# A QKV projection on one core: the first two row tiles of x loaded, cast and turned one by one, and the next work re-ordered around them

## Chip, cores, metric

One core of one Trainium2 chip. The metric is the device time of one execution in microseconds (us).

## The reference

```python
# x: 16 x 512 x 768 fp32, w_qkv: 768 x 2304 fp32
qkv = np.matmul(x, w_qkv)
q, k, v = qkv[..., :768], qkv[..., 768:1536], qkv[..., 1536:]
return np.stack([q, k, v], axis=0).astype(np.float32)
```

x is 8192 rows of 768 columns. A "row tile" is 128 rows, a "pair" two of them; there are 32 pairs. The 768 inner columns are six k-tiles of 128.

## The kernel before

The kernel has a start, which this change touches, and a long even part, which it does not. In the even part (pairs 3 to 31) the products are done in a seven-product scheme on 2 x 2 blocks, with TensorE nearly always busy. At the start the weights for that scheme are not there yet, so pairs 0 to 2 are multiplied plainly, block of weight columns by block, while the weights stream in. Rows of x must be cast to bf16 and turned (TensorE transposes through PSUM) before they can be a stationary operand. While nothing has landed, TensorE multiplies zeros ("warm-ups"), meant to have its clock at full rate when the work comes: in the trace of the kernel before these matmuls start 0.427 us apart at first and 0.216 us apart after 6.4 us.

```python
    def load_rows(p):                    # one load of 768 KB: a pair of x
        xin[p] = xin_pool.tile([P, 2, K], fp32, name="xin")
        rows = x_flat[p * 2 * P:(p + 1) * 2 * P, :]
        nc.sync.dma_start(xin[p][:], rows.rearrange("(r m) k -> m r k", m=P))

    def copy_halves(dst, src, two):      # VectorE takes a half, ScalarE the other
        nc.vector.tensor_copy(out=dst[0], in_=src[0])
        if two:
            nc.scalar.activation(dst[1], src[1], ident)
        else:
            nc.vector.tensor_copy(out=dst[1], in_=src[1])
    ...
    load_rows(0)
    ...
    load_rows(1)
    load_blocks(0, 0, 1)                 # six k-tiles of the first weight block, 256 KB each
    st_rem = o_pool.tile([P, KT, REM], fp32, name="str", tag="o")
    load_w(st_rem[:], 0, KT, R_OFF, REM) # weights of the 256 remainder columns, 768 KB
    load_rows(2)
    load_blocks(0, 1)
    ...
    busy(11)                             # warm-up matmuls on zeros
    cast_rows(0)
    turn_rows(0)
    busy(4)
    cast_rows(1)
    cast_k(0)
    cast_k(1)
    turn_rows(1)
    ...
    block(0, 0, b1[0], singles, nothing) # pairs 0 and 1 by the first weight block
    rem(0)                               # remainder columns of pair 0, 12 matmuls
    rem(1)
    cast_rows(2, False)
    turn_rows(2, False)
    block(0, 0, b1[0], halves((4, 5)), nothing)   # pair 2
    ...                                  # second weight block: never idle from here on
```

The schedule is written by hand: each engine runs its instructions in the order of the program. All loads shown go out on SyncE's queue.

## Time and profile before

| | before |
|---|---|
| time, median of 6 runs (those beside the changed kernel) | 362.96 us (362.75 to 363.25) |
| profiled span | 361.4 us |
| second pair of x has landed | 7.03 us |
| third pair of x has landed | 15.31 us |
| first product (TensorE) | 9.19 us |
| first product with the second weight block | 20.54 us |

The landings are read from the trace, which records when each load's semaphore is raised. The prediction below shows the page, the chain and the timeline. One more view: the table by stretches. Its columns are the stretch in us, its length, then for each engine the busy time and the number of instructions (PE, PEld, DVE, ACT, POOL), then the granted clock of TensorE, the mean busy share of the 16 DMA engines, and what they moved in GB/s.

### The profile page before, as it was taken

What the parts mean: (1) busy time and instruction counts of PE and PEld (TensorE: products, weight loads), DVE (VectorE), ACT (ScalarE), POOL (GpSimd) and SP (SyncE); (2) the same over time, 40 slices, a digit from 0 to 9 for tenths busy, and PEclk for the clock granted to TensorE, in tenths of its full rate; (3) what the DMA queues carried; (4) which work ended last, traced back from release to release, by engine and by line L of the source; (5) the groups of instructions that cost most, each with busy time, mean ns of one, the idle gap of its engine ahead of it and who ended that gap; (6) DMA issues with size and microseconds to landing.
All of it is one profiled execution on the core that took longest, in us unless ns stands there. A gap on an engine that the chain in (4) does not pass through costs nothing.

```text
span 361.4 us, 5220 instructions
## 1 busy us (share of the span) xinstructions
PE 353.3 (98%) x1765; PEld 250.8 (69%) x1797; DVE 222.7 (62%) x239; ACT 182.5 (51%) x304; POOL 174.4 (48%) x180
## 2 busy tenths in 40 slices
PE   8999999999999999999999999999999999999994
PEld 3644577777777777777777777777777777777763
DVE  3489546666566765566675565676556676556642
ACT  4547555455454545454545444445545454545452
POOL 0000970566664445664445665444666444566410
PEclk9999999999999999999999999999999999999999
DMA  7999969799899989999999999898999998989766
GB/s 294 381 383 338 348 227 345 271 354 304 279 322 298 296 275 296 282 313 314 284 278 295 282 306 316 284 276 291 295 285 317 295 296 276 297 279 331 267 251 242
DMA packets 80617, 108.08 MB, mean 299 GB/s; under 512 B 4816, under 2 KB 60368, under 8 KB 80592
## 3 DMA queue, kind: packets, MB, share of 16 engines
q1 hardware_dynamic: 65184, 96.35, 82.3%
q10 hardware_dynamic: 15408, 11.41, 9.9%
q8 instruction: 14, 0.23, 0.3%
q14 instruction: 11, 0.09, 0.1%
HBM read 32.24 MB, written 75.50 MB: 298 GB/s over the span
## 4 chain that ended last, share of the span: by engine, by line
PE 96%; ACT 1%; issue 1%; ACTq 0%; DVE 0%
PE ps L206 75%; PE ps L256 11%; PE ps L382 9%; PE ps L362 1%; PE ps L161 1%; ACT o L237 0%; ACTq L297 0%; ACT xb L141 0%; ACT orem L311 0%; DVE xb L139 0%; ACT xc L141 0%; ACTq L313 0%; DVE zero L340 0%; ACTq L311 0%
## 5 line engine op out<-in xcount | busy, mean ns | idle before, releaser
L206 PE MATMUL ps<-t,s 128*128 128x512 f32 x696 | 173.8, 398 | 0.0
L206 PEld LDWEIGHTS ps<-t,s 128*128 128x128 f32 x696 | 130.7, 188 | 29.8
L169 POOL CAST xb<-xf 128x1536 bf16<-128x1536 f32 x29 | 46.4, 1601 | 167.7 <-DVE xf L124 167.7
L234 DVE TENSOR_TENSOR o<-o,ps 128x512 f32<-128x512 f32 x58 | 39.9, 688 | 87.6 <-ACT o L233 87.6
L124 DVE STREAM_TRANSPOSE xf<-xin 128x1536 f32<-128x1536 f32 x29 | 85.7, 2956 | 9.7 <-DMA xin<-in_x_dram 7.1
L206 PE MATMUL ps<-b,xb 128*128 128x512 bf16 x320 | 82.4, 380 | 1.5
L233 ACT ACTIVATE o<-ps 128x512 f32<-128x512 f32 x58 | 34.7, 598 | 44.3 <-PE ps L206 44.3
L206 PEld LDWEIGHTS <-xb 128*128 128x128 bf16 x348 | 31.7, 98 | 35.6 <-issue 7.6
L227 ACT ACTIVATE o<-ps 128x512 f32<-128x512 f32 x58 | 34.8, 600 | 40.0 <-PE ps L206 37.3
L240 DVE TENSOR_TENSOR o<-o,ps 128x512 f32<-128x512 f32 x58 | 39.9, 688 | 21.4 <-PE ps L206 20.2
L206 PE MATMUL ps<-b,s 128*128 128x512 f32 x174 | 48.7, 389 | 0.0
L256 PE MATMUL ps<-w_rem,xb 128*128 128x256 bf16 x384 | 47.2, 273 | 0.0
L237 ACT ACTIVATE o<-ps 128x512 f32<-128x512 f32 x58 | 34.7, 598 | 24.1 <-PE ps L206 21.3
L220 ACT ACTIVATE o<-ps 128x512 f32<-128x512 f32 x58 | 34.6, 597 | 23.8 <-DVE o L240 20.7
L256 PEld LDWEIGHTS <-xb 128*128 128x128 bf16 x384 | 37.4, 98 | 11.2 <-issue 0.5
L224 DVE TENSOR_TENSOR o<-o,ps 128x512 f32<-128x512 f32 x58 | 36.5, 673 | 3.4 <-PE ps L206 2.1
L206 PEld LDWEIGHTS ps<-b,s 128*128 128x128 f32 x174 | 32.7, 188 | 6.8
L178 POOL TENSOR_TENSOR s<-s,xf 128x384 fp32r<-128x384 f32 x29 | 29.5, 1016 | 2.3
L266 ACT ACTIVATE orem<-ps 128x512 f32<-128x512 f32 x31 | 18.6, 598 | 22.7 <-PE ps L256 21.4
L179 POOL TENSOR_TENSOR s<-xf 128x384 fp32r<-128x384 f32 x29 | 29.5, 1017 | 0.0
L181 POOL TENSOR_TENSOR s<-xf,s 128x384 fp32r<-128x384 f32 x29 | 29.4, 1015 | 0.0
L177 POOL TENSOR_TENSOR s<-xf 128x384 fp32r<-128x384 f32 x29 | 29.3, 1012 | 0.0
(36 smaller groups left out, 127.2 us busy)
## 6 DMA issues: line engine op xcount, KB each, us to landing
out_dram<-o SPq DMA_DIRECT2D x62, 768.0 KB, 5.1
out_dram<-o SPq DMA_DIRECT2D x65, 256.0 KB, 4.6
xin<-in_x_dram SPq DMA_DIRECT2D x62, 192.0 KB, 6.7
xin<-in_x_dram ACTq DMA_DIRECT2D x54, 192.0 KB, 4.5
out_dram<-orem SPq DMA_DIRECT2D x31, 256.0 KB, 5.5
st<-in_w_qkv_dram SPq DMA_DIRECT2D x6, 768.0 KB, 14.1
xin<-in_x_dram SPq DMA_DIRECT2D x3, 768.0 KB, 5.8
st<-in_w_qkv_dram SPq DMA_DIRECT2D x6, 256.0 KB, 6.3
```

The source lines that it names most:

```text
L124: nc.vector.transpose(t[:].rearrange("p j (g b) -> p g j b", b=G), xin.pop(p)[:].rearrange("p g (a j) -> p g j a", a=G),)
L169: nc.gpsimd.tensor_copy(out=xb[p][:], in_=xf[p][:])
L206: nc.tensor.matmul(ps[:], lhs[j], rhs[j], start=(start and j == 0), stop=(j == KH - 1), skip_group_check=True,)
L220: nc.scalar.activation(c11, u.x[:], ident)
L224: nc.vector.tensor_tensor(c11, c11, u.z[:], op=add)
L227: nc.scalar.activation(c12, u.x[:], ident)
L233: nc.scalar.activation(c22, u.x[:], ident)
L234: nc.vector.tensor_tensor(c22, c22, u.y[:], op=add)
L237: nc.scalar.activation(c21, u.x[:], ident)
L240: nc.vector.tensor_tensor(c12, c12, u.y[:], op=add)
L256: nc.tensor.matmul(ps, xb[p][:, j, r * P:(r + 1) * P], w_rem[:, j, :], start=(j == 0), stop=(j == KT - 1), skip_group_check=True,)
L382: nc.tensor.matmul(ps[n][:], xb[p][:, j, r * P:(r + 1) * P], w[:, j, :], start=(j == 0), stop=(j == KT - 1), skip_group_check=True,)
```

## The change

The intent is to start sooner. The first row tile arrives alone, so that its cast and turn can begin a microsecond earlier; the second pair's first row is turned before its second; its second turn is put behind the two products with the first k-tile; the remainder's weights come in two halves and VectorE alone casts them; and each remainder is followed by the cast and turn of one row of the third pair. The core of the diff:

```diff
+    def load_row(p, r):
+        if r == 0:
+            xin[p] = xin_pool.tile([P, 2, K], fp32, name="xin")
+        row = (2 * p + r) * P
+        nc.sync.dma_start(xin[p][:, r, :], x_flat[row:row + P, :])
 ...   (cast_rows and turn_rows become cast_row and turn_row, one row tile each)
-    load_rows(0)
+    load_row(0, 0)
 ...
+    load_row(0, 1)
     load_rows(1)
-    load_blocks(0, 0, 1)
+    for j in range(KT):
+        load_k(j)
-    load_w(st_rem[:], 0, KT, R_OFF, REM)
+    for h in range(2):
+        load_w(st_rem[:, h * KH:(h + 1) * KH], h * KH, KH, R_OFF, REM)
 ...
-    busy(11)
-    cast_rows(0)
-    turn_rows(0)
-    busy(4)
-    cast_rows(1)
-    cast_k(0)
-    cast_k(1)
-    turn_rows(1)
+    busy(8)
+    cast_row(0, 0)
+    cast_row(0, 1)
+    turn_row(0, 0)
+    busy(1)
+    turn_row(0, 1)
+    busy(5)
+    cast_row(1, 0)
+    cast_row(1, 1)
+    cast_k(0)
+    turn_row(1, 0)
+    # products of k-tile 0 with pair 0, then: cast_k(1), turn_row(1, 1), the other casts
 ...
-    rem(0)
-    rem(1)
-    cast_rows(2, False)
-    turn_rows(2, False)
-    block(0, 0, b1[0], halves((4, 5)), nothing)
+    for p in range(2):
+        rem(p)
+        cast_row(2, p, False)
+        turn_row(2, p, False)
+    block(0, 0, b1[0], [(range(KT), (4, )), (range(KT), (5, ))], nothing)
```

More of the change, by code (lines that the diff above doesn't have):

```diff
@@ L145, with cast_row, turn_row @@
     xc = {}
-    def cast_rows(p, two=True):
-        src = xin.pop(p)
-        xc[p] = s_pool.tile([P, 2, K], bf16, name="xc", tag="s")
-        for r in range(2):
-            halves = (slice(0, K // 2), slice(K // 2, K))
-            copy_halves([xc[p][:, r, n] for n in halves], [src[:, r, n] for n in halves], two)
-    def turn_rows(p, two=True):
-        c = xc.pop(p)
-        xb[p] = xb_pool.tile([P, KT, 2 * P], bf16, name="xb")
-        for r in range(2):
-            cols = c[:, r, :].rearrange("m (p j) -> m j p", j=KT)
-            ps = ps_pool.tile([P, KT, P], bf16, name="ps")
-            for j in range(KT):
-                nc.tensor.transpose(ps[:, j, :], cols[:, j, :], eye)
-            ks = (slice(0, KH), slice(KH, KT))
-            copy_halves(
-                [xb[p][:, n, r * P:(r + 1) * P] for n in ks], [ps[:, n, :] for n in ks], two
-            )
+    def cast_row(p, r, two=True):
+        if r == 0:
+            xc[p] = s_pool.tile([P, 2, K], bf16, name="xc", tag="s")
+        halves = (slice(0, K // 2), slice(K // 2, K))
+        copy_halves([xc[p][:, r, n] for n in halves], [xin[p][:, r, n] for n in halves], two)
+    def turn_row(p, r, two=True):
+        if r == 0:
+            xb[p] = xb_pool.tile([P, KT, 2 * P], bf16, name="xb")
+        cols = xc[p][:, r, :].rearrange("m (p j) -> m j p", j=KT)
+        ps = ps_pool.tile([P, KT, P], bf16, name="ps")
+        for j in range(KT):
+            nc.tensor.transpose(ps[:, j, :], cols[:, j, :], eye)
+        ks = (slice(0, KH), slice(KH, KT))
+        copy_halves(
+            [xb[p][:, n, r * P:(r + 1) * P] for n in ks], [ps[:, n, :] for n in ks], two
+        )
     def round_x(p):
@@ L346, with load_k @@
     make_identity(nc, eye)
+    st_0 = tq_pool.tile([P, KT, CB], fp32, name="st0", tag="tq")
+    stage[0, 0, 0], stage[0, 1, 0] = st_0[:, :KH, :], st_0[:, KH:, :]
+    def load_k(j):
+        load_w(st_0[:, j:j + 1], j, 1, Q_OFF[0], CB)
+    load_row(0, 1)
     load_rows(1)
-    load_blocks(0, 0, 1)
+    for j in range(KT):
+        load_k(j)
     st_rem = o_pool.tile([P, KT, REM], fp32, name="str", tag="o")
-    load_w(st_rem[:], 0, KT, R_OFF, REM)
+    for h in range(2):
+        load_w(st_rem[:, h * KH:(h + 1) * KH], h * KH, KH, R_OFF, REM)
     load_rows(2)
-    load_blocks(0, 1)
+    load_blocks(0, 1, KH)
     load_blocks(1, 0)
@@ L375, in block @@
         ps = {}
-        for js, tiles in groups:
+        for group in groups:
+            if callable(group):
+                group()
+                continue
+            js, tiles = group
             for n in tiles:
@@ L396, in halves @@
         return [(range(h * KH, (h + 1) * KH), tiles) for h in range(2)]
-    singles = [((0, ), (0, 1)), ((1, ), (0, 1)), ((0, 1), (2, 3))]
-    singles += [((j, ), range(4)) for j in range(2, KT)]
     act, dve = nc.scalar, nc.vector
-    def cast_k(j):
-        dve.tensor_copy(out=b1[0][:, j, :], in_=stage[0, j // KH, 0][:, j % KH, :])
     def cast_next(q, c, w):
@@ L412, with fourth_row @@
     nothing = lambda p: None
-    busy(11)
-    cast_rows(0)
-    turn_rows(0)
-    busy(4)
-    cast_rows(1)
-    cast_k(0)
-    cast_k(1)
-    turn_rows(1)
-    for j in range(2, KT):
-        cast_k(j)
-    act.activation(w_rem[:, KH:], st_rem[:, KH:], ident)
-    dve.tensor_copy(out=w_rem[:, :KH], in_=st_rem[:, :KH])
+    busy(8)
[7 more added lines that the diff above has]
+    cast_row(1, 1)
+    cast_k(0)
+    turn_row(1, 0)
+    def fourth_row():
+        cast_k(1)
+        turn_row(1, 1)
+        for j in range(2, KT):
+            cast_k(j)
+        for h in range(2):
+            ks = slice(h * KH, (h + 1) * KH)
+            dve.tensor_copy(out=w_rem[:, ks], in_=st_rem[:, ks])
     bt0 = bt_pool.tile([P, KT, CB], bf16, name="bt")
     bt1 = bt_pool.tile([P, KT, CB], bf16, name="bt")
-    block(0, 0, b1[0], singles, nothing)
-    rem(0)
-    rem(1)
-    cast_rows(2, False)
-    turn_rows(2, False)
-    block(0, 0, b1[0], halves((4, 5)), nothing)
+    block(
+        0, 0, b1[0],
+        [((0, ), (0, 1)), fourth_row, ((1, ), (0, 1)), ((0, 1), (2, )), ((0, 1), (3, ))]
+        + [((j, ), range(4)) for j in range(2, KT)],
+        nothing,
+    )
+    for p in range(2):
[3 more added lines that the diff above has]
+    block(0, 0, b1[0], [(range(KT), (4, )), (range(KT), (5, ))], nothing)
     for h in range(2):
```

## The prediction

> **What bounds the kernel now.** I read the page first, for the engine that sets the pace, then its chain of work that ended last, then that chain in order of time for the first 21 us, which is the only stretch the change touches, and last the timeline by engine there.
>
> ```profile
> PE 353.3 (98%) x1765; PEld 250.8 (69%) x1797; DVE 222.7 (62%) x239; ACT 182.5 (51%) x304; POOL 174.4 (48%) x180
> ...
> PE 96%; ACT 1%; issue 1%; ACTq 0%; DVE 0%
> ```
>
> TensorE is busy 98% of a span of 361.4 us and carries 96% of the chain. So a change is worth what it moves TensorE's uninterrupted stream of work. The table by stretches has TensorE busy 23.36 of the 23.46 us from 20.54 us (the first product with the second block of weights) to 44 us; VectorE comes next with 19.10, and the chain there is matmuls alone. Whatever is won or lost before 20.54 us is carried unchanged to the end. The chain in order of time, 6 to 21 us (start, length, what):
>
> ```profile
> 6.06 0.59 PE ps L161 x6
> 6.65 0.02 issue
> 6.67 0.37 DVE xb L139
> 7.04 0.02 issue
> 7.07 0.87 ACT xb L141 x2
> 7.94 0.42 ACT xc L141
> 8.36 0.05 issue
> 8.40 0.95 PE ps L161 x12
> 9.35 2.16 PE ps L382 x10
> ...
> 14.53 2.62 PE ps L256 x24
> 17.15 0.35 PE ps L161 x6
> 17.50 0.02 issue
> 17.53 0.37 DVE xb L139
> 17.89 0.05 issue
> 17.94 0.39 PE ps L382
> ```
>
> L161 are the turns (PE transposes) of x, L382 the products of the first blocks, L256 those of the remainder columns. The reader is to see one long detour off TensorE, 6.65 to 8.40 us: ScalarE must copy the first pair's turned halves (0.87 us) before it casts the second pair, and TensorE stands still for the 0.57 us that the timeline gives ahead of the second turn. From 8.40 us on TensorE is on the path again and waits only once, about 0.28 us before 17.94.
>
> The timeline shows two loads that will matter (start, length, engine, what, idle before it):
>
> ```profile
> 7.04 0.39 SPq L135 DMA_DIRECT2D xin<-in_x_dram  x1
> 13.37 0.56 DVE L424 CAST w_rem<-str 128x768 bf16<-128x768 f32 x1 [1.83 <-DMA str<-in_w_qkv_dram]
> 15.43 0.36 DVE L139 CAST xc<-xin 128x384 bf16<-128x384 f32 x1 [1.50 <-DMA xin<-in_x_dram]
> ```
>
> VectorE sits idle 1.5 us until the third pair of x lands and casts it from 15.43 us. Issued at 7.04 us with 8.3 us to landing (the view of that tile), it lands at 15.3. The transfers run at 375 to 390 GB/s with the DMA share over 1.0 in these stretches, so it lands when the bytes queued ahead of it are through, not when it is asked for.
>
> **What the Trainium skill says.** "DMA: Bandwidth & Descriptors", section "Queues, rings and completion order": on each DMA engine descriptors are consumed in the order of the ring. The trace agrees: on this one queue the loads land in issue order, first pair of x at 5.05 us, second at 7.03, six k-tiles of weights 0.66 to 0.69 us apart from 7.72 to 11.09, the remainder weights at 13.35, third pair at 15.31. "TensorE: Matmul & The Clock Gate", Part 1: the array starts at half rate and is let go after a sustained busy window of about 3.4 us. The trace agrees in kind: the warm-up matmuls start 0.427 us apart, and in the middle of the first turns, at 6.4 us, spacing drops (turns 0.107 to 0.055 us, products 0.2155 us afterwards). The PEclk column shows 1.00 all through and does not show it. "PSUM — Partial Sum Buffer", section on bank collisions: VectorE and ScalarE must be kept apart on one bank. The trace agrees: each row's two half-copies out of PSUM run one after the other (0.36 then 0.49 us), while the two half-casts from SBUF run side by side.
>
> **The change part by part.**
>
> Loads. The first pair comes as two loads of 384 KB. By the packets, 384 KB are through about 1.0 us before 768 KB at 400 GB/s, so row 0 lands at about 4.05 us (estimate: 5.05 minus 0.99) and row 1 at 5.05 as now. The bytes ahead of the second pair, of every k-tile, of the remainder and of the third pair are the same: those land where they land now. The two loads more cost SyncE about 0.45 us each, hidden; it is seconds ahead of the data.
>
> First pair. Row 0: casts 4.07 to 4.59 (ScalarE's half, 0.52, is the longer). Eight warm-up matmuls end at 1.19 + 8 x 0.427 = 4.60, so turn 0 runs 4.64 to 5.28 at the slow rate (6 x 0.107). One warm-up to 5.71. Row 1's cast ends at 5.60, so turn 1 runs 5.71 to 6.35. VectorE copies row 1 at 6.58 to 6.94 (end of the last turn plus 0.3), ScalarE to 7.46.
>
> Second pair. It lands at 7.03. ScalarE, free at 7.46 and overlapping 0.12 with its next instruction, casts 7.34 to 7.87 and 7.76 to 8.28, in place of 7.82 to 8.76. So the turn of row 2 starts at about 7.92, in place of 8.40: a gain of 0.48 us here.
>
> First block. Turn of row 2 to 8.30; k-tile 0 is cast 7.74 to 8.16, so its two products run 8.30 to 8.73; turn of row 3 to 9.07. VectorE: copy of row 2 at 8.49, then k-tile 1 at 8.77 to 9.19, so the two products with it run from about 9.24 (0.17 us of stall). Copy of row 3 by VectorE 9.27 to 9.63, by ScalarE to 10.15, as tile 3 needs it at 10.10: 0.1 at most. From there the products are unbroken: 2 more, then 16 x 0.2155 = 3.45, to about 14.0 or 14.1. Now the remainder begins at 14.37. The gain at this point is 0.3 to 0.4 us.
>
> Remainder and third pair: here I expect the gain to be lost. The remainder's weights are cast by VectorE in two halves, the second 13.37 to 13.93, just in time. The new order is remainder of pair 0 (12 x 0.109 = 1.31), cast and turn of row 4, remainder of pair 1, cast and turn of row 5. The first remainder ends at 15.35. Row 4 can't be cast before the third pair lands: 15.43 to 16.06. TensorE takes its queue in order, so it waits about 0.7 us. Then from 16.10: turn 0.37 to 16.47; remainder of pair 1 to 17.78. VectorE copies row 4 out 16.66 to 17.28, then casts row 5 to 17.82, so the turn starts at 17.87, 0.09 late, and ends at 18.23. Twelve products at 0.2155 = 2.59: 20.82. In the kernel before this is 20.54 (14.37 + 2.62 + 0.66 + 0.28 + 2.59, which checks). The sum is +0.28 us; if the cast follows its landing by the usual 0.03 us rather than 0.12, +0.2.
>
> The old order had 2.62 us of remainder work to run while the third pair was being cast; the new one has half of that, and starts it earlier.
>
> **The rivals.** (1) The gain at the start is kept. For it: if the third pair landed by 14.6 us, no wait would be there, and the end of the stage would be 14.05 + 5.87 of work + about 0.1 = 20.0, so -0.5 us, 362.4. Against it: the same 4.7 MB precede its end at a full queue. (2) The clock gate opens a window later, since two slow turns with small gaps now fall into the stretch before 6.4 us where pure matmuls stood. Then products would run 0.427 us apart up to about 9.8 us and the first block would end near 15.1; the wait for the third pair swallows most of it, and the end is +0.5 us, 363.4. For it: I can't see the gate's threshold; against: TensorE is idle under 0.1 us from 1.19 to 6.35. (3) Row 0 lands later than 4.05 because a load has a fixed part. A delay of 0.3 us moves turn 0 but row 1's turn hangs on its own landing at 5.05; nothing after 7 us changes. (4) Another bound after 20.54, for instance VectorE's sums of weights: the weights for the second block's first half are cast by 19.6 us now, and need to be by 20.54; the new order puts that cast at 19.0 to 19.9. No effect.
>
> **Range and chances.** The stage's arrival at 16.10 fixes the middle: 362.89 + 0.2 or 0.28, so 363.1 us. Runs of the kernel before spread by 0.26 us. The low end, 362.4, is rival 1 in full; the high end, 363.7, is rival 2 with that spread. 2% is 7.3 us, more than the whole 9.2 us stretch before the first product could give back, as 1.3 us of it are turns and the first x can't land before 4 us. Within 2%: 0.98; faster 0.01; slower 0.01.
>
> **What would show it.** In the changed profile: turn of row 2 at 7.9 us; remainder from about 14.05; a wait of TensorE of some 0.7 us near 15.4, released by VectorE's or the load's row 4; the first product with the second block at 20.7 to 20.8. No wait near 15.4, or the third pair's cast before 15 us, would prove the central step wrong; products 0.43 us apart after 8.5 us would show rival 2; a later stage with new waits would show a bound that I have missed.

## More of the kernel before

The kernel before, 4 to 8 us:

```profile
4.00:5.00 1.00, 1.00 (x3) 0.30 (x2) 0.00 (x0) 0.00 (x0) 0.00 (x0) 1.00 1.01 406
5.00:6.00 1.00, 1.00 (x5) 0.42 (x4) 0.63 (x2) 0.92 (x2) 0.00 (x0) 1.00 1.03 418
6.00:7.00 1.00, 1.00 (x14) 0.91 (x13) 0.33 (x1) 0.01 (x1) 0.00 (x0) 1.00 1.03 400
7.00:8.00 1.00, 0.83 (x4) 0.20 (x2) 1.00 (x5) 0.94 (x3) 0.00 (x0) 1.00 1.06 404
```

The last number of each line is what the reader is to keep: 400 to 418 GB/s without a dip.

## The result, and the profile after

The changed kernel takes 365.03 us (median of 6 runs, 364.81 to 365.76) beside 362.96 us for the kernel before. The ratio is 1.0062, with an interval of 1.0049 to 1.0075. The change is 2.1 us slower: within 2%, as forecast, but outside the range of 362.4 to 363.7.

The page of the changed kernel, the lines that answer to the first fence of the prediction:

```profile
PE 354.4 (97%) x1764; PEld 251.4 (69%) x1796; DVE 223.0 (61%) x240; ACT 182.4 (50%) x303; POOL 174.4 (48%) x180
...
PE 95%; DMA 2%; ACT 1%; issue 1%; ACTq 0%; SPq 0%
```

The profiled run is one of the two slowest of the six (365.67 us). A DMA now stands in the chain that ended last, with 2% of 363.9 us. The chain in order of time for the changed kernel says which (start, length, what; L165 are turns, L400 products of the first blocks, L260 the remainder):

```profile
1.65 7.52 DMA xin<-in_x_dram
9.17 0.02 issue
9.19 0.53 ACT xc L147
9.72 0.05 issue
9.77 0.84 PE ps L165 x6
10.61 0.85 PE ps L400 x2
11.47 0.64 PE ps L165 x6
12.11 2.40 PE ps L400 x9
...
17.32 1.31 PE ps L260 x12
18.63 0.33 PE ps L165 x6
18.96 1.31 PE ps L260 x12
20.27 0.48 PE ps L165 x6
```

The load issued at 1.65 us is the second pair of x, and it lands at 9.17 us, not at 7.03. In the kernel before this load is not in the chain at all. The same stretches as above, changed kernel:

```profile
4.00:5.00 1.00, 1.00 (x6) 0.55 (x5) 0.12 (x1) 0.28 (x1) 0.00 (x0) 1.00 0.92 264
5.00:6.00 1.00, 1.00 (x8) 0.51 (x7) 0.64 (x2) 0.67 (x2) 0.00 (x0) 1.00 0.88 304
6.00:7.00 1.00, 1.00 (x10) 0.65 (x9) 0.36 (x1) 0.50 (x2) 0.00 (x0) 1.00 0.91 243
7.00:8.00 1.00, 0.49 (x3) 0.00 (x0) 0.00 (x0) 0.34 (x1) 0.00 (x0) 1.00 0.97 341
...
9.00:10.00 1.00, 0.23 (x3) 0.23 (x4) 0.76 (x3) 0.81 (x2) 0.00 (x0) 0.75 1.04 393
10.00:11.00 1.00, 1.00 (x8) 0.71 (x7) 0.64 (x3) 0.13 (x1) 0.00 (x0) 0.50 1.05 398
```

Two things are to be seen. From 4 to 8 us the DMA engines move 243 to 341 GB/s in place of 400 to 418. And from 9.5 us the granted clock is 0.50: TensorE stands idle for 2.28 us up to 9.77, and meanwhile its clock is halved again. The timeline of TensorE has that wait, and where the stage ends (start, length, instruction, idle before it):

```profile
9.77 0.84 PE L165 MATMUL ps<-eye,xc 128*128 128x128 bf16 x6 [2.28 <-ACT xc L147]
...
23.18 3.19 PE L400 MATMUL ps<-bt,xb 128*128 128x512 bf16 x14
```

The same two places in the kernel before:

```profile
8.40 0.95 PE L161 MATMUL ps<-eye,xc 128*128 128x128 bf16 x12 [0.57 <-ACT xc L141]
...
20.54 7.93 PE L382 MATMUL ps<-bt,xb 128*128 128x512 bf16 x36
```

The loss is made in this stage and carried on: the first product with the second weight block comes at 23.18 us in place of 20.54, 2.64 us late, and the profiled spans differ by 2.5 us.

**Where the 2.1 us in the load come from.** The Trainium skill, "DMA: Bandwidth & Descriptors", section "Why a DMA increments its semaphore by 16 and not by 1", says that up to 16 DMA engines carry a load and finish independently, each raising the semaphore by one. So the trace holds 16 times for each load. Its record of landings, in us, with the median engine as the ninth of the 16 to finish:

| load | kernel | median engine | 15th to finish | last engine |
|---|---|---|---|---|
| second pair of x | before | 6.84 | 7.01 | 7.03 |
| second pair of x | changed | 6.73 | 8.70 | 9.17 |
| k-tile 0 | before | 7.52 | 7.69 | 7.72 |
| k-tile 0 | changed | 7.95 | 9.39 | 9.85 |
| third pair of x | before | 15.13 | 15.29 | 15.31 |
| third pair of x | changed | 15.69 | 16.96 | 17.43 |

In the kernel before the last engine is within 0.2 us of the median. In the changed one the median engine has its share of the second pair sooner than before, and the last is 2.4 us behind it. The lag is still there eight microseconds later: at the third pair the last engine is 1.74 us behind the median one, and 2.12 us later than in the kernel before, as it was 2.14 us late for the second pair. Single pieces show it too: among those that start between 0 and 10 us, 16 took over 0.2 us in the kernel before, all of them started before 2.8 us; in the changed kernel there are 53, up to 8.9 us, the longest 1.41 us for 3 KB that otherwise take 0.12.

One rival can be put aside from the same record: a piece of instructions that takes an engine away. In the kernel before one such piece, 16 KB on a queue of its own, takes 1.10 us from 18.65 us on, and in the four weight loads that land after it, 20.84 to 26.86 us, the last engine is 1.4 to 1.5 us behind the 15th. So one engine's delay does carry over from load to load; but in no run does a piece of instructions start between 0 and 18 us, so this isn't what happens at the start.

### The profile page after: what moved, and what is told of

Read it like the earlier page. It is cut to its first block, busy times and chain, and to the rows that moved or that the text cites. A ratio compares the mean times of both kernels' runs of the same rounds, so it can differ in the third digit from the quotient of the medians.

```text
span 363.9 us, 5219 instructions
## 1 busy us (share of the span) xinstructions
PE 354.4 (97%) x1764; PEld 251.4 (69%) x1796; DVE 223.0 (61%) x240; ACT 182.4 (50%) x303; POOL 174.4 (48%) x180
## 4 chain that ended last, share of the span: by engine, by line
PE 95%; DMA 2%; ACT 1%; issue 1%; ACTq 0%; SPq 0%
PE ps L210 74%; PE ps L260 11%; PE ps L400 9%; DMA xin<-in_x_dram 2%; PE ps L165 1%; ACT o L241 0%; ACTq L301 0%; SPq L136 0%; ACT orem L315 0%; ACT xc L147 0%; ACTq L317 0%; ACTq L315 0%
## 5 line engine op out<-in xcount | busy, mean ns | idle before, releaser
L260 PE MATMUL ps<-w_rem,xb 128*128 128x256 bf16 x384 | 47.3, 273 | 0.0
L260 PEld LDWEIGHTS <-xb 128*128 128x128 bf16 x384 | 37.4, 98 | 11.2 <-issue 0.5
```

The costliest lines, as they stand in the source:

```text
L260: nc.tensor.matmul(ps, xb[p][:, j, r * P:(r + 1) * P], w_rem[:, j, :], start=(j == 0), stop=(j == KT - 1), skip_group_check=True,)
```

## The experiments

Sixteen kernels ran. Each was timed beside the kernel before on the same chip, whose medians were 362.7 to 363.1 us throughout. "Second pair" and "third pair" are the landings in the profiled run.

| run | edit, on which kernel | median us | ratio to before, interval | second pair | third pair |
|---|---|---|---|---|---|
| one_load | changed; first pair in one load | 363.36 | 1.0019 (1.0004 to 1.0034) | 7.13 | 15.40 |
| split_only | before; first pair in two loads | 365.46 | 1.0069 (1.0041 to 1.0096) | 8.92 | 17.21 |
| warm | changed; 15 warm-ups, not 5 | 364.78 | 1.0054 (1.0039 to 1.0069) | 8.68 | 16.95 |
| rem_one | changed; remainder's weights in one load | 364.98 | 1.0053 (1.0036 to 1.0070) | 9.11 | 17.41 |
| part_halves | before; first pair by partition halves | 364.97 | 1.0062 (1.0047 to 1.0077) | 8.97 | 17.25 |
| second_split | before; second pair in two loads | 363.03 | 1.0009 (0.9992 to 1.0026) | 7.37 | 15.62 |
| both_split | before; both pairs in two loads | 364.14 | 1.0038 (1.0023 to 1.0053) | 8.88 | 17.17 |
| act_queue | before; two loads on two queues | 362.88 | 1.0003 (0.9988 to 1.0018) | 6.91 | 15.19 |
| late_cast | split_only; second row cast first | 364.37 | 1.0034 (1.0017 to 1.0052) | 8.94 | 17.21 |
| act_after | changed; two loads on two queues | 363.19 | 1.0011 (0.9994 to 1.0027) | 6.88 | 15.15 |
| short_head | before; k-tile 0 ahead of the first pair | 363.36 | 1.0012 (0.9995 to 1.0028) | 7.56 | 15.18 |
| strided_rows | split_only; every second row (wrong result) | 363.76 | 1.0027 (1.0013 to 1.0042) | 8.57 | 16.84 |
| col_halves | before; first pair by column halves | 362.93 | 1.0010 (0.9994 to 1.0027) | 8.64 | 16.96 |
| two_short | before; k-tiles 0 and 1 ahead | 367.53 | 1.0131 (1.0117 to 1.0144) | 10.96 | 17.89 |
| act_best | act_after; remainders and turns re-ordered | 362.75 | 0.9992 (0.9977 to 1.0007) | 6.99 | 15.26 |
| act_best5 | the same again, 5 rounds | 362.71 | 0.9996 (0.9982 to 1.0010) | 6.85 | 15.12 |

### Is it the two loads, the clock, or the other loads?

**one_load** undoes only the split of the first pair; **split_only** does only that split.

```diff
 # one_load, on the changed kernel            # split_only, on the kernel before
-    load_row(0, 0)                           -    load_rows(0)
+    load_rows(0)                             +    load_row(0, 0)
 ...                                          ...
-    load_row(0, 1)                           +    load_row(0, 1)
     load_rows(1)                                  load_rows(1)
```

> The changed kernel with the first pair of x in one load again, all else of the change kept. Theory A (the two loads of the first pair slow the transfers behind them: the second pair landed at 9.17 us in place of 7.03): the second pair lands near 7.0 us, the third near 15.3, TensorE waits about 0.7 us ahead of the turn of row 4, the first product with the second block comes at 20.7 to 20.9, and the time is 363.1 to 363.3, about 1.8 us under the changed kernel. Theory B (the other loads or the new order cause the slow transfers, or the chip did by chance): the second pair still lands near 9 us and the time stays at 364.8 to 365.8.

> The kernel before with nothing changed but the first pair of x in two loads of a row tile. Theory A: the second pair lands near 9 us, the turn of the second pair starts near 9.8 us in place of 8.40, and the time is 364.3 to 365.7. Theory B: it lands at 7.0 and the time stays within 0.3 us of 363.0.

Both came out as theory A has it. Without the split the second pair lands at 7.13 us and the time is 363.36 us, 1.7 us less than the changed kernel's but still clear of the kernel before; with nothing but the split the kernel before takes 365.46 us, and its timeline of TensorE has the same wait as the changed kernel's:

```profile
9.52 0.95 PE L167 MATMUL ps<-eye,xc 128*128 128x128 bf16 x12 [2.20 <-ACT xc L147]
```

What ends last in that run is another late load, the remainder's weights, which land at 15.26 us in place of 13.35. split_only's runs fall in two groups: 364.20 and 364.66 us (the profiled one), and 366.25 and 366.32 us with a mean granted clock of 0.993. The profiles in which the clock is seen to fall again have 0.994 or 0.995, so a second fall is a likely part of the difference; it is not shown.

Two expectations of one_load missed: in its profiled run there is no wait ahead of the turn of row 4, and the first product with the second weight block comes at 21.75 us, not 20.7 to 20.9. That run, at 364.26 us, was the slowest of its four (the others 363.29 to 363.36). Its timeline tells why:

```profile
5.78 0.84 PE L165 MATMUL ps<-eye,xc 128*128 128x128 bf16 x6 [1.00 <-ACT xc L147]
...
7.48 2.34 PE L374 MATMUL ps<-zero 128*128 128x512 bf16 x5
```

Eight warm-ups end a microsecond before the first row of a whole pair is cast (it lands at 5.18 us), and the five warm-ups from 7.48 us still take 2.34 us, at the slow rate. The clock was let go only at 9.77 us, where the trace's record of the granted clock begins; the clock column of the tables prints 1.00 before that for want of a record. That is the prediction's rival 2, here through an idle stretch that it had not foreseen.

**warm** and **rem_one** test the rivals on the changed kernel.

```diff
-    busy(5)        # warm
+    busy(15)
```

> The changed kernel with 15 warm-up matmuls in place of 5 ahead of the second pair, so that TensorE has no long idle stretch and its clock is not halved again. Theory C (the second fall of the clock is the loss): about 1.4 us of the 2.1 us comes back, 363.5. Theory A: the third pair still lands near 17.4 us and holds TensorE, so at most 0.3 us comes back, 364.6 to 365.0, with a new wait of about 1 us ahead of the turn of row 4.

> The changed kernel with the remainder's weights in one load, as before. Theory A: no difference, 364.8 to 365.5, the second pair still lands near 9 us. Theory B (the number of loads in flight slows the transfers): the second pair lands earlier and the time falls towards 363.

The second fall of the clock is not the loss. In warm the clock stays at 1.00, and the median is 0.25 us below the changed kernel's (against the kernels before beside them, 1.0054 and 1.0062, with intervals that overlap). The changed kernel's own runs agree: going by their mean clock, it fell again in two of the six, 365.67 us (the profiled run, 0.995) and 365.76 us (0.993). The other four, at 0.997 to 0.999, took 364.81 to 365.20 us, still 1.8 to 2.2 us above the kernel before. What the warm clock wins is spent waiting for the third pair, as theory A has it. Its timeline:

```profile
15.36 1.47 PE L260 MATMUL ps<-w_rem,xb 128*128 128x256 bf16 x12
17.77 0.54 PE L165 MATMUL ps<-eye,xc 128*128 128x128 bf16 x6 [0.93 <-DVE xc L149]
18.14 1.47 PE L260 MATMUL ps<-w_rem,xb 128*128 128x256 bf16 x12
```

The remainder of pair 0 ends early and TensorE stands 0.93 us until VectorE has cast row 4. This is the wait that the prediction put at 15.4 us; it ends 1.7 us later (17.77 for 16.10) because the third pair lands at 16.95 us, not 15.31. In rem_one, with one load fewer, nothing changes: the number of loads in all is not the cause.

### What about the two loads?

Now the kernel before serves as the base, since split_only shows the harm there alone.

**late_cast**: is it the early casts and turns, which use the on-chip memory while the loads run? The two rows of the first pair are cast in the other order, so nothing is touched before the second load has landed.

> The kernel before with the first pair in two row-tile loads, as in split_only, but its second row tile cast first, so that VectorE and ScalarE touch nothing before the second load has landed. Theory W (the early casts and turns, which read and write the on-chip memory while the loads run, slow them): no harm, second pair near 7.0 us, time near 363.0. Theory S (the loads themselves): second pair near 9 us as in split_only, time 364.2 to 366.3.

It is not: the second pair lands at 8.94 us, the time is 364.37 us.

**act_queue**: both row tiles at the same moment, the second from ScalarE's queue.

```diff
-    load_rows(0)
+    load_row(0, 0)
+    load_row(0, 1, nc.scalar)
```

> The kernel before, first pair as two row-tile loads, the second of them issued from ScalarE's queue at the same moment as the first from SyncE's, so that the DMA engines alternate between the two row tiles. Theory R: normal, second pair near 7.0 us, time within 0.4 us of 362.9. Theory S: slow as the changed kernel, second pair near 9 us.

No harm: the rows land at 4.72 and 4.89 us, the second pair at 6.91, the time is 362.88 us. **second_split** and **both_split** move the split.

> The kernel before, first pair whole, second pair in two row-tile loads. Theory S (short load at the head of the program): no harm, the k-tiles land from 7.7 us on as before, time within 0.3 us of 362.9. Theory R: the slow stretch follows here too, k-tile 0 lands 1 us or more late, time 363.9 or more.

> The kernel before, both first pairs in row-tile loads. Theory M (the harm comes from a whole-pair load running behind row-tile loads, the two orders meeting in memory): no harm, second pair complete near 7.0 us, time within 0.3 us of 362.9. Theories S and R: second pair complete near 9 us, 364.2 to 365.7.

Behind a whole first pair the split does little: the second pair is complete 0.34 us late (7.37), and the time is not to be told from the kernel before. Split both pairs, and the harm is there in full (8.88 us), so it is not a whole-pair load running behind row tiles: theory M falls.

**part_halves** loads the first pair as partitions 0 to 63 and 64 to 127.

> The kernel before, first pair in two loads by partitions (64 partitions, both row tiles, each): the same 384 KB and the same 3 KB pieces per load as the row-tile loads, but row tiles interleaved as in the whole pair. Theory S (a short load at the head, whatever its order, spoils the transfers behind it): the second pair lands near 9 us, time 364.2 to 365.7. Theory R (it is the order of x's rows, one tile after the other): lands near 7.0 us, time within 0.3 us of the kernel before.

The number fits theory S, but the run does not decide: its first 384 KB alone landed only at 5.04 us, and for the second pair its median engine (8.65) is nearly as late as its last (8.97). All engines are slow, not one. It is another harm than the changed kernel's.

**short_head** and **two_short** put one and two k-tiles of the weights (256 KB each) ahead of the first pair, which stays whole.

> The kernel before with the first k-tile of the weights (256 KB) loaded ahead of the first pair, which stays whole. Theory S in its general form (any short load at the head of the queue spoils what follows): the first pair lands at 5.7 us but the second at 9 or later in place of 7.7, time 364.5 or more. If it takes a short load of x itself: second pair at 7.6 to 7.8 us, time 363.2 to 363.8.

> short_head with two k-tiles of the weights ahead of the first pair, 128 pieces of 2 KB each. Theory L by number of pieces: the pairs land at 6.4 and 8.4 us if normal, but 10 us or more for the second if L holds, time over 365. Theory U: normal, 8.4 us, time 363.8 to 364.5 (0.7 us of weights more ahead of the first pair).

One short load at the head does nothing: the second pair lands at 7.56 us, the time is 363.36. Two do the most harm of all: 8.56 and 10.96 us for the two pairs, 367.53 us. So it does not take x, nor a row tile. **strided_rows** and **col_halves** change the shape of the two loads of x.

> split_only with each load taking every second row of the first 256, so the same 128 pieces of 3 KB per load but no unbroken stretch of memory; the rows of the first pair come out in the wrong places on purpose, the result is wrong. Theory U (the unbroken 384 KB stretch is what spoils it): second pair near 7.0 us, time near 363.0. Theory L (two loads of 128 pieces at the head): near 9 us, 364.2 to 366.3.

> The kernel before with the first pair in two loads by column halves, each with all 256 rows, 256 pieces of 1.5 KB. Theory L by number of pieces, and theory U: normal, second pair near 7.0 us, time 362.6 to 363.3. Theory L by bytes (384 KB is too short): near 9 us, 364.2 or more.

strided_rows has no unbroken stretch of memory, and is slow, though less so (363.76 us) and not in every run: 364.25 (profiled) and 364.58 us, but also 363.25 and 363.28. Theory U falls all the same. In the profiled run, 15 engines have their share of the second pair at 7.19 us and the last at 8.57, while the DMA rate hardly dips (372 to 392 GB/s from 4 to 8 us): a single engine behind is enough. col_halves is between: its profiled run (364.34 us) has the second pair at 8.64 us, but the other three runs (362.68 to 363.17 us) can hardly have had that delay in full. With 256 pieces to each load the harm comes and goes, so the number of pieces in a load does not decide alone.

What is shown: two short loads, one behind the other on one queue, at the head of the program, leave one or some of the 16 engines 1.4 to 2.4 us behind in the profiled runs (by column halves and by every second row not in all runs, as far as their times tell). One short load, whole pairs, or the same two loads on two queues do not. The second queue also lets both short loads go out at once and the second pair at 1.18 us in place of 1.65. In short_head the second pair goes out at 1.65 us too, without harm, so its time of issue alone is not the cause; but whether the queue or the gap between the two short loads matters no run tells. Why an engine falls behind is left open. No run shows what the slow pieces wait for.

### A version without the harm

**act_after** is the changed kernel with row tile 1 on ScalarE's queue; **act_best** also puts both remainders and both casts of the third pair ahead of its turns, with 10, 1 and 4 warm-ups.

> The changed kernel with one edit: row tile 1's load issued from ScalarE's queue at the start. If the two loads on one queue are the whole of the loss, the second pair lands near 6.9 us, the third near 15.2, TensorE waits 0.6 to 0.9 us ahead of the turn of row 4, the first product with the second block is at 20.5 to 20.8 us, and the time is 362.7 to 363.3, some 2 us under the changed kernel. If not, it stays above 364.4.

> The same with both remainders ahead of the turns of the third pair, as in the kernel before, and 10, 1 and 4 warm-up matmuls. If the order of the remainders is what costs the early start, there is no wait ahead of row 4, the first product with the second block is at 20.1 to 20.3 us and the time is 0.3 us under the kernel before, 362.3 to 362.6. If the early start isn't real, within 0.1 us of the kernel before or above it.

> The same kernel as act_best, more rounds. If the gain is real: 0.3 us under the kernel before, ratio 0.9990 with an interval below 1. If not, the interval holds 1.

act_after takes back all that can be told from noise: 363.19 us, 363.09 beside it. Its timeline:

```profile
8.41 0.54 PE L165 MATMUL ps<-eye,xc 128*128 128x128 bf16 x6 [0.20 <-ACT xc L147]
...
14.48 1.47 PE L260 MATMUL ps<-w_rem,xb 128*128 128x256 bf16 x12
15.96 0.54 PE L165 MATMUL ps<-eye,xc 128*128 128x128 bf16 x6
```

The turn of row 2 is at 8.41 us, no sooner than in the kernel before, since the clock opened late in this run (the five warm-ups took 1.39 us) and held up the chain of turn, copy and cast; so the remainder began late, and the wait for row 4 is not there to be seen. act_best brings the first product with the second weight block to 19.84 us in one profiled run and to 20.29 in the other, against 20.54, and its medians are 0.1 to 0.3 us below the kernel before; both intervals hold 1. A gain of that size may be real; it is not shown.

## Why the prediction was wrong, point by point

- **What bounds the kernel, and that the stage before 20.54 us decides all**: right. That product came 2.64 us late and the span grew by 2.5 us.
- **Row 0 lands at about 4.05 us, row 1 at 5.05; turns at 4.64 and 5.71**: right to about 0.3 us. They landed at 3.73 and 5.15, the turns began at 4.58 and 5.75. For row 1 this is luck: 15 of its 16 engines were done at 4.66 us, and only the last, already behind, brought the landing near 5.05.
- **"The bytes ahead ... are the same: those land where they land now"**: this is the step that failed. The bytes and their order were the same, and the loads still landed 2.1 us later, because a load has landed only when the slowest of 16 engines has, and the two short loads left some engines behind. I had read in the trace of the kernel before that loads land in order and at full rate, and took the landing to be bytes over rate; I had not asked how even the 16 engines were, and listed no rival in which the transfers themselves slow down. split_only shows the cause by itself, one_load and act_after take it away.
- **The gain of 0.48 us at the turn of the second pair**: never came about, as it hung on a landing at 7.03. With the harm removed and the clock open, act_best's two profiled runs began that turn at 7.59 and 8.05 us; I had 7.92.
- **The third pair holds TensorE in the new order of remainders**: right in kind. warm shows it (0.93 us) and rem_one has it too (0.53 us); in the profiled run of the changed kernel the halved clock made the remainder begin late enough to hide it.
- **Rival 2, the clock**: it did fall again, but through the 2.28 us wait, not through the turns. It costs time of its own (from the turn of row 2 to the remainder 7.39 us in place of 5.97) but most of that lies beside the wait for the third pair: in rem_one, with the third pair at 17.41 us (17.43 here) and the clock at 1.00, the first product with the second weight block comes at 22.98 us, only 0.20 us sooner.
- **"hidden; it is seconds ahead of the data"**, of SyncE's issue: microseconds are meant, and the third pair's issue hangs on earlier landings. It went out at 7.04 us, right after the second pair had landed (7.03), and now at 9.86, right after k-tile 0 (9.85); as it lands 7.6 us after that, the loads ahead of it still set its landing.
- **The sum**: with the failed step undone, one_load and act_after take 363.36 and 363.19 us, in the range and near the 363.1 that was named. But the wait ahead of row 4 was in neither profiled run, so they do not prove that sum term by term. Of the miss of 1.9 us, undoing the lag takes back 1.7 and 1.8.

## What to carry to other kernels

A load ends with its slowest DMA engine, so bytes over rate gives its landing only while the engines keep step. After a change at the head of a queue, look at the spread between the median and the last of the 16 landings, not at the rate alone: here the engines that fell behind were still behind 8 us later. Where a first load is to be split, try its parts on two queues before giving the split up: here that took the harm away, though it won nothing clear of noise.

## What the Trainium skill lacked or had wrong

- "DMA: Bandwidth & Descriptors" says that the engines of a load finish independently. It lacks how far apart they can drift and how long that lasts under a full queue: 2.4 us between the median and the last engine for the second pair, and 1.7 us still there at the third, 8 us later.
- The same page lacks any note on the pattern that sets it off: two loads of 256 to 384 KB one behind the other at the head of one queue (365.46 and 367.53 us; by column halves mostly not, 362.93), but not one short load (363.36), nor two on two queues (362.88). Its advice on size, to batch loads for efficiency, would have pointed the right way but does not name this: the loads were not slow themselves (rows at 3.73 and 5.15 us), those behind them were.
- The same page says that loads from several queues share the same 16 engines and only the issue time is saved. Here the load behind landed at 6.91 us with the second queue and at 8.92 without, 2.0 us apart, while its issue came only 0.47 us sooner; the gap between the two short loads went with it, so the queue by itself is not shown to do it.
- "TensorE: Matmul & The Clock Gate" says that the clock falls back after an idle window of about 3.4 us. Here a wait of 2.28 us was enough in the changed kernel (clock 0.50 from 9.5 us), while 2.20 us in split_only was not in the profiled run. The traces' record of the clock tells them apart: it fell in three runs, each time 3.41 or 3.42 us after it had opened, and TensorE was busy for 1.41 us of that stretch in the changed kernel, 1.19 in part_halves and 0.28 in two_short. In the first 3.41 us after its opening rem_one was busy for 1.46 us and split_only for 1.94, and there it did not fall, though rem_one's wait was 2.38 us. So in these five runs the fall goes with the busy time of the stretch, not with the length of the wait. That it opens at a time that varies with the run agrees with the page: in these profiles between 4.4 us (act_queue) and 9.8 us (one_load, with a wait of 1.00 us on the way), with TensorE at work from 1.19 us in each. Even without one_load, up to 7.2 us (both_split), the spread is wider than the 0.5 us either way that the page gives.
